# Hybrid trunk layer on one core: the joint turns of two up-projection pairs placed behind the product of the third quarter

## The chip, the cores and the metric

The kernel runs on one core of one Trainium2 chip. The metric is the device time of one execution in microseconds (us). The core's engines are TensorE (PE, with its weight loads, PEld, as a row of their own), VectorE (DVE), ScalarE (ACT), GpSimd (POOL) and SyncE (SP, which issues most DMAs). Each has its own queue and runs it in order; they wait for each other through semaphores.

## The reference

One layer of a trunk on 256 tokens of width 2048: a norm, a gated delta rule and a pooling mixer behind one input projection, an output projection, and then a feed-forward part. The change is in the feed-forward part's up projection.

```python
h = rmsnorm(x, norm_ffn_w[l])
gate, up = jnp.split(jnp.einsum('bsd,df->bsf', h, w_up[l]), 2, axis=-1)      # w_up: 2048 x 2*5632
gate = causal_dwconv(gate, conv_ffn_w[l]) + conv_ffn_b[l]                    # three taps over the tokens
x = x + jnp.einsum('bsf,fd->bsd', jax.nn.gelu(gate, approximate=False) * up, w_down[l])
...
return rmsnorm(x, norm_final_w)
```

## The kernel before

**Numbers.** Every float32 weight tile (128 partitions x 2 x 512) is split in two tiles of a shorter type: a high half, cast by ScalarE (`whi`, L318), and a low half, the difference, made by VectorE (`wlo`, L329). Activations are split in the same way. A product of two such operands is three matmuls: high with high, high with low, low with high.

**Tiling of the up projection.** The 5632 columns are 11 chunks of 512 (`c` = 0 to 10), each with a gate half and an up half: a pair. For each pair there are four results of 128 tokens x 512 columns: `bank[col, t]`, column half `col` (0 gate, 1 up) and token half `t`. The contraction of 2048 is eight steps `kp` of 256. In a "plain" step one weight tile meets both token halves, twelve matmuls. A "group" replaces four plain steps (two `kp`, gate and up), which are eight quarter products of six matmuls each, by seven such products on sums of weight quarters and sums of activation quarters. Its products are named 11, T1, T2, 21, T3, 22 and T4. Pairs 1 to 7 and 9 have two groups each (chunks in `TWO`); pairs 8 and 10 have one.

**How the seven products share results.** Some results are begun as copies or sums of others. T1 has a bank of its own ("own"), which ScalarE copies out. When 21 is reached, VectorE adds `bank[0, 1]` and "own" into `bank[1, 0]` (L1438); T3 accumulates into that same `bank[0, 1]`; behind T3 VectorE adds `bank[0, 1]` and "own" again into `bank[1, 1]` (L1459). Product 22 goes into `bank[1, 0]`, T4 into `bank[1, 1]`, 21 into `bank[0, 0]`. The matmuls of products and plain steps are all at L1423.

**Turns.** When the last plain step of a column half is done, ScalarE copies its two banks to an `e` tile (L1473 for gate, L1476 for up). The "turns" of chunk `c` are 16 transposes on TensorE (L1485), eight of the gate `e` and eight of the up `e`, each into a two-bank tile of the pool `psm` (two tiles). Then `gate_part` runs the three taps on the turned gate (L1370 on ScalarE, L1375 on VectorE) and the Gelu, and `up_part` multiplies with the turned up (L1391) and splits the result.

**What sets the order.** TensorE's order is written out by hand: the list `up_steps`, built pair by pair, is walked under a manual schedule for PE. While chunk `c` ends, the group of chunk `c + 1` begins: its products stand between the last up steps (`rest`) of chunk `c`, and the turns of chunk `c` stand among them. The queues of the other engines follow from a scheduler and from the order in which the work is issued. Up to three `whi` and three `wlo` tiles are alive, four raw weight tiles, and four banks of the pool `psg`.

Of the kernel before, what the change touches and what calls it, by code (L numbers as in the profile page):

```python
# [36 lines left out]
def kernel(  # L37
# [63 lines left out]
    up_steps = []  # L101
    TAIL = 3
    for c in range(NUP):
        kps = [kp for kp in range(KD // 2) if kp // 2 not in chunks_of[c]]
        gate_steps, up_only = ([("plain", c, col, kp) for kp in kps] for col in range(2))
        tail = min(6, len(kps)) if c + 1 in TWO else TAIL
        up_steps += gate_steps[:tail]
        for a, b in zip(gate_steps[tail:], up_only):
            up_steps += [a, b]
        rest = up_only[-tail:]  # L110
        if c + 1 == NUP:
            up_steps += rest
            break
        parts = [[("part", c + 1, what, ch) for what in UP_PARTS] for ch in chunks_of[c + 1]]
        if len(rest) == 4:
            up_steps += [rest.pop(0)]
        up_steps += [("loads", c + 1)]
        if c + 1 in TWO:
            first_four = [parts[ch][n] for ch in range(2) for n in (0, 1)] + [parts[ch][2] for ch in range(2)]
            if len(rest) == 3:  # L120
                rest = rest[:2] + [None] + rest[2:] + [None, None]
            for a, b in zip(first_four, rest):
                up_steps += [a, b] if b else [a]
            p21, t3, p22, t4 = ([parts[ch][n] for ch in range(2)] for n in range(3, 7))
            up_steps += p21 + t3 + p22 + [("turns", c)] + t4
        else:
            t1, p11, t2, p21, t3, p22, t4 = parts[0]
            up_steps += [t1, rest[0], p11, rest[1], t2, rest[2], p21, t3, p22, ("turns", c), t4]
    for step in up_steps:
        if step[0] == "plain":  # L130
            srcs.append(up_w[step[1]][step[2]][step[3]])
# [1438 lines left out]
    for hf in range(2):  # L1570
# [11 lines left out]
        for n, step in enumerate(steps[hf]):  # L1582
# [9 lines left out]
            if step[0] == "plain":  # L1592
                kp, c = step[1], step[2] % 2
# [147 lines left out]
```

## Time and profile before

| | |
|---|---|
| median of 3 runs | 1536.62 us (1535.81 to 1536.63) |
| profiled execution | 1536.34 us |
| its span | 1534.6 us |
| granted TensorE clock, mean | 0.998 |
| busy: PE, PEld, DVE, ACT | 99%, 82%, 81%, 57% of the span |
| 16 transposes of a chunk (L1485) | 64 matmuls for the chunks 6 to 9 between 1100 and 1300 us |

The span is what the profiler saw of the one execution; 1.74 us lie outside it. Times in rows are microseconds from the span's start. In a row of the timeline stand start, duration, engine, line, operation, output and inputs; in square brackets, where there are any, the engine's idle time just before and what ended it. A duration of several merged instructions (x4) goes from the first one's start to the last one's end. The rows of a weight load show best when TensorE turns to the next product.

### The profile page before, as it was taken

What the parts mean: (1) busy time and instruction counts of PE and PEld (TensorE: products, weight loads), DVE (VectorE), ACT (ScalarE), POOL (GpSimd) and SP (SyncE); (2) the same over time, 40 slices, a digit from 0 to 9 for tenths busy, and PEclk for the clock granted to TensorE, in tenths of its full rate; (3) what the DMA queues carried; (4) which work ended last, traced back from release to release, by engine and by line L of the source; (5) the groups of instructions that cost most, each with busy time, mean ns of one, the idle gap of its engine ahead of it and who ended that gap; (6) DMA issues with size and microseconds to landing.
All of it is one profiled execution on the core that took longest, in us unless ns stands there. A gap on an engine that the chain in (4) does not pass through costs nothing.

```text
span 1534.6 us, 20205 instructions
## 1 busy us (share of the span) xinstructions
PE 1522.4 (99%) x7290; PEld 1255.5 (82%) x7290; DVE 1235.9 (81%) x1729; ACT 871.3 (57%) x1126; POOL 71.5 (5%) x97
## 2 busy tenths in 40 slices
PE   9999999999999999999999999999999999999997
PEld 8878888788888888788888888888888888888876
DVE  6779758885589757877667999999998886989896
ACT  6455446454556446454455676666766665555553
POOL 1000000000000001000000000000000011010200
PEclk9999999999999999999999999999999999999999
DMA  8777658776667656766578646666456568566662
GB/s 278 208 228 211 191 152 232 223 201 172 199 213 218 186 160 208 231 192 192 177 259 302 197 163 216 219 208 218 151 188 210 150 219 264 173 220 209 235 203 97
DMA packets 170098, 313.61 MB, mean 204 GB/s; under 512 B 23650, under 2 KB 27010, under 8 KB 169870
## 3 DMA queue, kind: packets, MB, share of 16 engines
q1 hardware_dynamic: 160864, 283.17, 59.3%
q0 software_dynamic: 7344, 27.27, 5.4%
q10 hardware_dynamic: 1790, 1.89, 0.4%
q8 instruction: 57, 0.93, 0.3%
q14 instruction: 43, 0.35, 0.1%
HBM read 303.33 MB, written 8.95 MB: 203 GB/s over the span
## 4 chain that ended last, share of the span: by engine, by line
PE 98%; DVE 1%; issue 0%; ACT 0%; DMA 0%; POOLq 0%; POOL 0%; SPq 0%; DVEq 0%; ACTq 0%
PE psg L1423 28%; PE psm L368 15%; PE psm L366 15%; PE psm L367 15%; PE psm L1408 7%; PE psg L1408 7%; PE psm L1423 2%; PE psm L512 1%; PE psm L1485 1%; PE psg L411 1%; PE psg L899 1%; DVE wlo L329 0%; PE psg L901 0%; ACT whi L318 0%; PE psg L1037 0%
## 5 line engine op out<-in xcount | busy, mean ns | idle before, releaser
L318 ACT CAST whi<-raw 128x1024 fp32r<-128x1024 f32 x420 | 440.7, 1052 | 408.3 <-PE psm L367 252.2
L329 DVE TENSOR_TENSOR wlo<-raw,whi 128x1024 fp32r<-128x1024 f32 x418 | 509.8, 1224 | 166.8 <-ACT whi L318 160.6
L318 ACT CAST whi<-quad 128x1024 fp32r<-128x1024 f32 x182 | 191.1, 1054 | 140.5 <-PE psg L1423 46.4
L329 DVE TENSOR_TENSOR wlo<-quad,whi 128x1024 fp32r<-128x1024 f32 x182 | 221.2, 1223 | 28.8 <-ACT whi L318 27.5
L368 PE MATMUL psm<-wlo,xhl 128*128 128x512 f32 x432 | 170.2, 394 | 0.2 <-DVE wlo L329 0.2
L366 PE MATMUL psm<-whi,xhl 128*128 128x512 f32 x432 | 169.0, 391 | 0.0
L367 PE MATMUL psm<-whi,xhl 128*128 128x512 f32 x432 | 168.6, 390 | 0.0
L1423 PE MATMUL psg<-whi,fhl 128*128 128x512 f32 x504 | 127.2, 390 | 0.0
L1423 PEld LDWEIGHTS psg<-whi,fhl 128*128 128x128 f32 x504 | 94.4, 188 | 19.5
L368 PEld LDWEIGHTS psm<-wlo,xhl 128*128 128x128 f32 x432 | 81.1, 188 | 17.9 <-DVE wlo L329 1.1
L367 PEld LDWEIGHTS psm<-whi,xhl 128*128 128x128 f32 x432 | 81.1, 188 | 16.6
L366 PEld LDWEIGHTS psm<-whi,xhl 128*128 128x128 f32 x432 | 81.2, 188 | 16.5
L245 DVE TENSOR_TENSOR quad<-quad,quad 128x1024 f32<-128x1024 f32 x72 | 87.9, 1221 | 0.0
L1423 PE MATMUL psg<-wlo,fhl 128*128 128x512 f32 x252 | 69.8, 389 | 0.0
L1423 PE MATMUL psg<-whi,ups 128*128 128x512 f32 x216 | 58.0, 390 | 1.5 <-DVE psg L1438 1.5
L1423 PEld LDWEIGHTS psg<-wlo,fhl 128*128 128x128 f32 x252 | 47.3, 188 | 9.9
L1408 PE MATMUL psm<-whi,hhi 128*128 128x512 f32 (+1 forms) x140 | 54.3, 388 | 0.1
L1408 PE MATMUL psm<-whi,hlo 128*128 128x512 f32 (+1 forms) x140 | 54.1, 386 | 0.0
L1408 PE MATMUL psm<-wlo,hhi 128*128 128x512 f32 (+1 forms) x140 | 53.9, 386 | 0.0
L366 PE MATMUL psm<-whi,mhi 128*128 128x512 f32 x128 | 50.8, 397 | 0.0
L368 PE MATMUL psm<-wlo,mhi 128*128 128x512 f32 x128 | 50.0, 390 | 0.0
L367 PE MATMUL psm<-whi,mlo 128*128 128x512 f32 x128 | 49.9, 390 | 0.0
(439 smaller groups left out, 2918.4 us busy)
## 6 DMA issues: line engine op xcount, KB each, us to landing
raw<-in_w_in_dram SPq DMA_DIRECT2D x224, 512.0 KB, 4.3
raw<-in_w_up_dram SPq DMA_DIRECT2D x104, 512.0 KB, 4.8
quad<-in_w_up_dram SPq DMA_DIRECT2D x72, 512.0 KB, 4.7
raw<-in_w_down_dram SPq DMA_DIRECT2D x56, 512.0 KB, 5.2
raw<-in_w_out_dram SPq DMA_DIRECT2D x32, 512.0 KB, 4.0
quad<-in_w_down_dram POOLq DMA_DIRECT2D x32, 512.0 KB, 5.6
mv<-vrow SPq DMA_DIRECT2D x12, 512.0 KB, 4.8
taps<-in_conv_qkv_w_dram SPq DMA_DIRECT2D x16, 256.0 KB, 5.7
```

The costliest lines, as they stand in the source:

```text
L245: nc.vector.tensor_tensor(out_, plus_, minus_, op=ALU.subtract)
L318: last_cast[0] = nc.scalar.copy(hi, raw).ins
L329: last_split[0] = nc.vector.tensor_tensor(lo, raw, hi.bitcast(F32), op=ALU.subtract).ins
L366: mm(ps[:, t, :], lh(k, t), hi[:, kk, :], start=(k == 0), stop=False)
L367: mm(ps[:, t, :], ll(k, t), hi[:, kk, :], start=False, stop=False)
L368: mm(ps[:, t, :], lh(k, t), lo[:, kk, :], start=False, stop=(k == nk - 1))
L411: nc.tensor.transpose(pt[:, ff, t * P : (t + 1) * P], src[:, t, f * P : (f + 1) * P], ident)
L512: mm(ps_k0[:, t, :], part(k, t), w[:, kk, :], start=(k == 0 and w is hi and part is xh), stop=(k == KD - 1 and w is lo))
L899: mm(pg0, kq[:, h, 0, 0:P], kq[:, h, :, :], start=True, stop=True)
L1408: mm(ps[:, cs], lhs(kk), part_[:, kk, cs], start=(first and kk == 0 and n == 0), stop=(last and kk == 1 and n == 2), skip_group_check=shared)
L1423: mm(ps, lhs(kk), w[n][:, kk], start=(first and n == 0 and kk == 0 and lhs is high), stop=False, skip_group_check=True)
L1485: nc.tensor.transpose(out_[f // 2][:, f % 2, t * P : (t + 1) * P], e[:, t, f * P : (f + 1) * P], ident)
```

## The change

In the two pairs with one group (the chunks 8 and 10) the turns of the chunk before stand directly behind product 21, ahead of T3 and 22. Before they stood behind 22, ahead of T4. The other pairs are as they were. Nothing is added or taken away.

```diff
         else:
             t1, p11, t2, p21, t3, p22, t4 = parts[0]
-            up_steps += [t1, rest[0], p11, rest[1], t2, rest[2], p21, t3, p22, ("turns", c), t4]
+            up_steps += [t1, rest[0], p11, rest[1], t2, rest[2], p21, ("turns", c), t3, p22, t4]
```

What this makes of the queues is shown at the first of the two places, the end of chunk 7 (the second, the end of chunk 9, has the same moves). The rows give line, operation, output and inputs; + is after, - before. On TensorE, from product 21 (bank `psg_10115`) on; `whi_10141` and `wlo_10143` are T3's weights, `whi_10164` and `wlo_10166` those of 22, `whi_10176` before that of T4:

```order
 L1423 MATMUL psg_10115<-whi_10117,fhl_6782 128x512 x4
 L1423 MATMUL psg_10115<-wlo_10119,fhl_6782 128x512 x2
+L1485 MATMUL psm_10176<-ident,e_10044 128x128 x8
+L1485 MATMUL psm_10185<-ident,e_10157 128x128 x8
 L1423 MATMUL psg_10108<-whi_10141,ups 128x512 x4
 L1423 MATMUL psg_10108<-wlo_10143,ups 128x512 x2
 L1423 MATMUL psg_10162<-whi_10164,ups 128x512 x4
 L1423 MATMUL psg_10162<-wlo_10166,ups 128x512 x2
-L1485 MATMUL psm_10202<-ident,e_10044 128x128 x8
-L1485 MATMUL psm_10211<-ident,e_10157 128x128 x8
```

The gate turns (`e_10044`) and the up turns (`e_10157`) moved ahead of T3 and 22; T4 now follows 22 directly.

On VectorE, from the add at 21 on (`wlo` of a quad is T4's low half, those of raw tiles belong to the first two plain steps of chunk 8):

```order
 L1438 TENSOR_TENSOR psg_10162<-psg_10108,own_10082 128x512
-L329 TENSOR_TENSOR wlo_10178<-quad_9926,whi_10176 128x1024
-L1459 TENSOR_TENSOR psg_10186<-psg_10108,own_10082 128x512
-L329 TENSOR_TENSOR wlo_10194<-raw_10190,whi_10192 128x1024
+L329 TENSOR_TENSOR wlo_10198<-quad_9926,whi_10196 128x1024
+L1459 TENSOR_TENSOR psg_10206<-psg_10108,own_10082 128x512
+L1375 SCALAR_TENSOR_TENSOR y_10254<-psm_10176,cfw,y_10254 128x255
+L329 TENSOR_TENSOR wlo_10212<-raw_10208,whi_10210 128x1024
+L1375 SCALAR_TENSOR_TENSOR y_10254<-psm_10176,cfw,y_10254 128x254
 L329 TENSOR_TENSOR wlo_10224<-raw_10220,whi_10222 128x1024
-L1375 SCALAR_TENSOR_TENSOR y_10254<-psm_10202,cfw,y_10254 128x255
-L1375 SCALAR_TENSOR_TENSOR y_10254<-psm_10202,cfw,y_10254 128x254
```

The low half of T4 and the two adds keep their places (only their buffers have other numbers); the first two taps of the gate moved ahead, each before a low half of a plain step.

On ScalarE, from the copies of up `e` on:

```order
 L1476 COPY e_10157<-psg_9840 128x512
 L1476 COPY e_10157<-psg_9884 128x512
-L318 CAST whi_10176<-quad_9926 128x1024
-L318 CAST whi_10192<-raw_10190 128x1024
+L318 CAST whi_10196<-quad_9926 128x1024
+L1370 ACTIVATE y_10254<-psm_10176,vec,cfw 128x256
+L318 CAST whi_10210<-raw_10208 128x1024
 L318 CAST whi_10222<-raw_10220 128x1024
-L1370 ACTIVATE y_10254<-psm_10202,vec,cfw 128x256
```

The first gate activation moved ahead of the high halves of two plain steps. The queues of SyncE and GpSimd keep their order.

## The prediction

> **What bounds the kernel now.** I read the page's first and fourth part first, then the waits of the two TensorE rows, then the chain of waits around each place that the change touches.
>
> ```profile
> span 1534.6 us, 20205 instructions
> ...
> PE 1522.4 (99%) x7290; PEld 1255.5 (82%) x7290; DVE 1235.9 (81%) x1729; ACT 871.3 (57%) x1126; POOL 71.5 (5%) x97
> ...
> PE 98%; DVE 1%; issue 0%; ACT 0%; DMA 0%; POOLq 0%; POOL 0%; SPq 0%; DVEq 0%; ACTq 0%
> ```
>
> TensorE carries 98% of the chain that ends last. So only two things can move the time: TensorE work taken away, or a hole on TensorE filled. The change takes no work away (16 transposes before, 16 after, in each pair). What is left is holes. The waits of matmuls (PE) and of weight loads (PEld), longest first, columns "us in total, times, longest":
>
> ```profile
> PE psg L1423 <- DVE psg L1438: 1.5, 2, 0.7
> ...
> PE psg L1423 <- DVE wlo L329: 0.5, 2, 0.3
> PE psg L1408 <- ACT whi L318: 0.4, 2, 0.2
> ...
> PEld psg L1423 <- DVE psg L1438: 2.3, 2, 1.2
> ```
>
> The largest entry among the matmul waits is one product waiting for the add of L1438, twice. L1438 makes bank[1, 0] from bank[0, 1] and "own" at the product 21; the product T3 then accumulates into the same bank[0, 1], so it must wait until the add has read it. The chain of waits, in order of time, shows where the two are:
>
> ```profile
> 1165.16 1.22 DVE wlo L329
> 1166.38 0.62 DVE psg L1438
> 1167.00 0.04 issue
> 1167.05 3.02 PE psg L1423 x12
> 1170.07 1.75 PE psm L1485 x16
> ...
> 1253.98 0.62 DVE psg L1438
> 1254.60 0.04 issue
> 1254.65 3.02 PE psg L1423 x12
> 1257.67 1.75 PE psm L1485 x16
> ```
>
> Both holes are in the two pairs of this change (chunks 8 and 10; the turns of L1485 there are those of chunks 7 and 9), two products ahead of the turns. The reader should see that the turns need nothing of this add: they read only the evicted e tiles.
>
> **The size of a hole.** I go by the starts of weight loads. The timeline of the first place (start, duration, engine, line; p21 is the load at 1164.55, T3 at 1167.04, 22 at 1168.31, the turns at 1169.67, T4 at 1171.54, the first plain product of chunk 8 at 1172.81):
>
> ```profile
> 1164.55 0.87 PEld L1423 LDWEIGHTS psg<-whi,fhl 128*128 128x128 f32 x4
> 1165.02 1.07 ACT L1476 COPY e<-psg 128x512 f32<-128x512 f32 x2
> 1165.98 1.06 ACT L318 CAST whi<-quad 128x1024 fp32r<-128x1024 f32 x1
> 1166.30 0.69 DVE L1438 TENSOR_TENSOR psg<-psg,own 128x512 f32<-128x512 f32 x1
> 1167.04 0.77 PEld L1423 LDWEIGHTS psg<-whi,ups 128*128 128x128 f32 x4 [1.17 <-DVE psg L1438]
> 1167.07 1.22 DVE L329 TENSOR_TENSOR wlo<-quad,whi 128x1024 fp32r<-128x1024 f32 x1
> 1168.28 1.05 ACT L318 CAST whi<-raw 128x1024 fp32r<-128x1024 f32 x1 [1.24 <-PE psg L1423]
> 1168.31 0.87 PEld L1423 LDWEIGHTS psg<-whi,ups 128*128 128x128 f32 x4
> 1168.74 0.70 DVE L1459 TENSOR_TENSOR psg<-psg,own 128x512 f32<-128x512 f32 x1 [0.45 <-PE psg L1423]
> 1169.36 2.59 DVE L329 TENSOR_TENSOR wlo<-raw,whi 128x1024 fp32r<-128x1024 f32 x2
> 1169.67 1.90 PEld L1485 LDWEIGHTS psm<-ident,e 128*128 128x128 f32 x16
> 1170.98 0.56 ACT L1370 ACTIVATE y<-psm,vec,cfw 128x256 f32<-128x256 f32 x1 [0.28 <-PE psm L1485]
> 1171.54 0.76 PEld L1423 LDWEIGHTS psg<-whi,fhl 128*128 128x128 f32 x4
> 1172.81 1.80 PEld L1423 LDWEIGHTS psg<-whi,fhl1a 128*128 128x128 f32 x8
> ```
>
> An undisturbed product of six matmuls holds TensorE for 1169.67 - 1168.31 = 1.36 us; the 16 turns for 1171.54 - 1169.67 = 1.87; the product right behind the turns for 1172.81 - 1171.54 = 1.27. From p21 to the first plain product TensorE takes 1172.81 - 1164.55 = 8.26 us. With p21 1.36, turns 1.87, T3 1.27, 22 1.36 and T4 1.36 it is 7.22. The hole is worth 1.04 us. The same stretches of the second place, p21, then T3 with its hole, the turns and T4 (us, PE busy, clock, DMA share, GB/s):
>
> ```profile
> 1252.15:1253.51 1.36, 1.36 (x7) 1.00 0.83 259
> 1253.51:1255.91 2.40, 1.65 (x7) 1.00 0.64 222
> ...
> 1257.27:1259.14 1.87, 1.87 (x17) 1.00 0.85 285
> 1259.14:1260.41 1.27, 1.27 (x9) 1.00 0.78 247
> ```
>
> They are equal to the first place to the hundredth: 2.40 where 1.36 was due, 1.04 again. The granted clock is 1.00 in all of them, so nothing comes or goes by the clock.
>
> A rule on how to read such a gap: the Trainium skill, "Perfetto Trace Analysis", section "Identifying the Most-Contended Engine", says that matmul busy time misjudges TensorE because matmuls are pipelined, and that weight-load busy time is the better measure. The two wait rows bear it out in part: matmul idle gives 1.5 us for both places, weight-load idle 2.3, the distance between starts 2.08. By that page alone the gain would be 2.3 and the time 0.2 lower than mine; the starts decide, because a load that follows a stall or the turns is 0.09 us shorter (1.27 against 1.36).
>
> **The change step by step.** *Turns ahead of T3, on TensorE:* they start when p21 is through, 1164.55 + 1.36 = 1165.91, and end at 1167.78. The add of L1438 is done at 1166.30 + 0.69 = 1166.99, and a load follows it 0.05 later (1167.04). So T3 finds its bank free 0.74 us early: the hole is gone, -1.04 in each pair. *What the turns themselves need:* gate e is old; the two copies of up e (L1476) end at 1165.02 + 1.07 = 1166.09, and the up turns, the second eight of 16, start at 1165.91 + 1.87/2 = 1166.85. Spare 0.76: no wait, 0.
>
> *What is late next: T4.* Before, the turns stood between 22 and T4 and covered L1459, the add that makes T4's bank from T3's result. That cover is gone. L1459 starts 1168.74 - 1167.04 = 1.70 after T3's load and takes 0.70. T3 now loads at 1167.78, L1459 runs 1169.48 to 1170.18, T4 may load at 1170.23. Its turn comes at 1167.78 + 1.27 + 1.36 = 1170.41. Spare 0.18: cost 0, but this is the tightest point of the forecast. L1459 cannot be held by VectorE: ahead of it stands only T4's low half, which is done at 1167.07 + 1.22 = 1168.29.
>
> *VectorE and ScalarE, new places in the queues.* On ScalarE y0 (L1370) now stands ahead of the first plain product's high half. It starts 1170.98 - 1169.67 = 1.31 after the turns, so at 1167.22, ends at 1167.78, while the high half behind it waits anyway until T3 has released its buffer: 1.24 after T3's load (1168.28 - 1167.04), so 1169.02. Cost 0. On VectorE one tap (L1375) now stands ahead of the first plain low half: L1459 ends 1170.18, the tap (0.48) 1170.66, the low half about 1171.85. TensorE loads that product at 1170.41 + 1.36 = 1171.77, and its low matmuls come 1.8 us into it (the row at 1172.81 loads eight high weights first), at 1173.57. Spare 1.7: cost 0. The row for the tap's length, and the rows for the loads:
>
> ```profile
> L1375 DVE SCALAR_TENSOR_TENSOR y<-psm,cfw,y x37: 474/478/484, 1099.8 to 1268.2; 128x254 f32<-128x254 f32 x19, 128x255 f32<-128x255 f32 x18
> ...
> 1170.62 30.73 SPq L224 DMA_DIRECT2D raw<-in_w_up_dram  x10
> ...
> 1183.94 1.98 PE L1423 MATMUL psg<-whi,fhl 128*128 128x512 f32 x8
> ...
> DMA to landing us min/median/max: 3.6/4.7/6.5
> ```
>
> *The SyncE queue.* Its order is unchanged, and no step issues a DMA, but the load issued at 1170.62, behind the first plain low half, refills that product's buffer for the fifth plain product (the matmul at 1183.94, so its load about 1183.7). It is issued about 1.25 us later now and wanted 1.04 earlier. Landing at 1171.9 + 6.5 = 1178.4 at the latest of these rows; wanted, with one cast of 1.05, by 1183.7 - 1.04 - 1.05 = 1181.6. Spare 3.2 us: cost 0. GpSimd's order does not change.
>
> *Sum:* 2 x -1.04 = -2.08 us. The profiled execution took 1536.34 us, 1.74 outside its span of 1534.6; it becomes a span of 1532.5 and 1534.26 in all. The median of the runs (1536.62) is 0.28 above the profiled one; against it the sum gives 1534.54, and I predict 1534.5. Everything behind 1173 only moves up with TensorE, which paces it.
>
> Bounds of what the trace before does not show, T4 directly behind 22: best, the whole -2.08; a little more if the shift also shortens one of the later small waits (I allow 0.3 for run to run); worst, T4 waits for L1459 a whole VectorE low half (1.22) longer, less its spare of 0.18, which is 1.04 and takes the gain away. The row nearest to the new order is L1459's own start 0.45 after VectorE fell idle, so I take no wait.
>
> **Rivals.** (1) T4 takes the wait over. For it: 0.18 us of spare. Against it: VectorE is idle ahead of L1459, so nothing can push it. From 0.18 of lateness on it costs one for one, at 1.22 nothing is left: 1534.6 to 1536.6. (2) The up turns wait for the copies of up e. Against it: 0.76 of spare; it needs a high-half cast (1.06) to slip ahead of the copies, for a loss of 0.3 in each pair: 1535.1. (3) Slower: the refill for the fifth plain product, issued later and wanted earlier, makes its cast late and TensorE waits. Issued at 1171.9 and wanted by 1181.6, it starts to cost when the load takes 9.7 us, gives no change at 10.7, and at 12.3 in both pairs (2.6 lost in each, 1.04 won) the kernel is at 1539.7. The longest of 37 loads took 6.5, so this wants a queue about twice as slow. (4) More than the sum: gate work that starts earlier also removes later waits, for below 1533.5; against it, the later matmul waits quoted above hold 0.5 + 0.4 us together, which is 1533.6 with all of them gone.
>
> **How the numbers follow.** Chances: the sum holds (within 0.4 us of 1534.5) 0.77; rival 1 0.09; rival 2 0.04; rival 3, or an unforeseen loss of that size, 0.04; rival 4 0.06. A measurement of this kernel can tell about 0.2%, 3.1 us, from no change; the sum is 0.135%. So within 0.2%: 0.77 + 0.09 + 0.04 = 0.90; faster by more 0.06; slower by more 0.04. The range runs from the fastest run less the sum (1535.81 - 2.08 = 1533.7, and 0.1 for spread) to 1536.7, where rival 1 has eaten everything.
>
> **What the changed profile would show.** Right: no waits for L1438 in either wait view; 7.2 us, not 8.26, from p21's first load to the first plain product in both pairs; T3 right behind the turns; VectorE idle some 1.2 us, not 0.45, ahead of L1459; the span near 1532.5. Wrong: a wait of T4 for L1459 (rival 1), of the turns for L1476 (rival 2), of a cast for a raw load about 14 us behind T3 with TensorE idle after it (rival 3). If the two stretches are 7.2 us and the span is not shorter, a wait further on gave the time back, and my claim that TensorE paces all that follows was the wrong step.

## The result and the profile after

| | before | after |
|---|---|---|
| median of 20 runs each | 1536.41 us (1535.48 to 1537.42) | 1533.84 us (1533.35 to 1534.79) |
| ratio, after to before | | 0.9985, 95% interval 0.9979 to 0.9991 |
| profiled execution | 1536.34 us | 1533.53 us |

By the medians the change is worth 2.57 us, by the ratio 2.3; the interval, times 1536.41, reaches from 1.4 to 3.2 us. The forecast was 2.08 us less and 1534.5 us. Faster, then, by 0.15%: less than the 0.2% that the prediction thought could be told from no change, but with 20 runs each the interval leaves out 1. In two later series one execution took far longer than all others (3121 us of the kernel before, 2573 us of the kernel with all pairs); without them the medians given below move by less than 0.1 us.

The lines of the page of the changed kernel that answer to those of before:

```profile
span 1531.8 us, 20205 instructions
...
PE 1521.9 (99%) x7290; PEld 1256.6 (82%) x7290; DVE 1235.4 (81%) x1729; ACT 871.7 (57%) x1126; POOL 71.1 (5%) x97
...
PE 98%; issue 0%; DVE 0%; ACT 0%; POOL 0%; POOLq 0%; ACTq 0%; DVEq 0%
```

The counts are the same, and the busy times differ by 0.5 us for matmuls and VectorE and by 1.1 us for weight loads; the span is 2.8 us shorter. No work went away, so idle time did. VectorE's share of the chain fell from 1% to 0%. All waits of matmuls that the view still lists (us in total, times, longest):

```profile
PE psm L427 <- POOL ones L417: 1.1, 1, 1.1
PE psg L1408 <- ACT whi L318: 0.4, 2, 0.2
PE psm L368 <- DVE wlo L329: 0.2, 1, 0.2
```

The largest entry of before in the up projection, 1.5 us for L1438, is gone, and none for L1459 or L1476 has come. (Two small entries of before are missing too, L1423 for low halves and L512 for a cast; both lie ahead of the two places and come and go between executions of the same code.) The chain of waits through the first place (start, duration, what) shows it as one unbroken run of TensorE:

```profile
1159.83 5.90 PE psg L1423 x26
1165.73 1.75 PE psm L1485 x16
1167.48 14.52 PE psg L1423 x64
```

Before, the add of L1438 stood in this chain as a link of 0.62 us between p21 and T3. The rows of the timeline that bear on the first place, others left out (p21 loads at 1163.97, the turns at 1165.34, T3 at 1167.21, 22 at 1168.47, T4 at 1169.83, the first plain product at 1171.19):

```profile
1163.97 0.87 PEld L1423 LDWEIGHTS psg<-whi,fhl 128*128 128x128 f32 x4
1164.44 1.07 ACT L1476 COPY e<-psg 128x512 f32<-128x512 f32 x2
1165.34 1.91 PEld L1485 LDWEIGHTS psm<-ident,e 128*128 128x128 f32 x16
1165.72 0.69 DVE L1438 TENSOR_TENSOR psg<-psg,own 128x512 f32<-128x512 f32 x1
1166.64 0.56 ACT L1370 ACTIVATE y<-psm,vec,cfw 128x256 f32<-128x256 f32 x1 [0.19 <-PE psm L1485]
1167.21 0.76 PEld L1423 LDWEIGHTS psg<-whi,ups 128*128 128x128 f32 x4
1168.47 0.87 PEld L1423 LDWEIGHTS psg<-whi,ups 128*128 128x128 f32 x4
1168.89 0.70 DVE L1459 TENSOR_TENSOR psg<-psg,own 128x512 f32<-128x512 f32 x1 [1.18 <-PE psg L1423]
1169.50 0.47 DVE L1375 SCALAR_TENSOR_TENSOR y<-psm,cfw,y 128x255 f32<-128x255 f32 x1
1169.83 0.87 PEld L1423 LDWEIGHTS psg<-whi,fhl 128*128 128x128 f32 x4
1171.19 1.77 PEld L1423 LDWEIGHTS psg<-whi,fhl1a 128*128 128x128 f32 x8
```

The add runs from 1165.72 to 1166.41, wholly beside the turns, and no weight load has a bracket behind it: no wait of TensorE is listed. From p21 to the first plain product it is 1171.19 - 1163.97 = 7.22 us, where it was 8.26. The second place by stretches (us, PE busy; the columns are those of before): p21, the turns, T3, 22 and T4:

```profile
1250.48:1251.84 1.36, 1.36 (x8) 1.13 (x6) 0.76 (x1) 1.36 (x3) 0.64 (x1) 1.00 0.76 253
1251.84:1253.71 1.87, 1.87 (x17) 1.77 (x16) 1.79 (x3) 1.68 (x3) 0.72 (x1) 1.00 0.82 269
1253.71:1254.97 1.26, 1.26 (x8) 1.06 (x7) 0.51 (x1) 0.03 (x2) 0.45 (x1) 1.00 0.69 241
1254.97:1256.33 1.36, 1.36 (x7) 1.13 (x6) 0.93 (x2) 1.05 (x2) 0.28 (x1) 1.00 0.83 295
1256.33:1257.69 1.36, 1.36 (x7) 1.13 (x6) 1.36 (x3) 1.06 (x2) 0.00 (x0) 1.00 0.75 241
```

TensorE is busy through each of them, at a granted clock of 1.00; they sum to 7.21 us.

**Where the 2.8 us of the spans come from.** Two stretches give 1.04 + 1.05 = 2.09. Another 0.58 is there before the place is reached (1163.97 against 1164.55), in instructions that both kernels issue in the same order; the rest is 0.1. The 0.58 is a balance of small waits that differ in both directions: just ahead of 963 us the changed kernel was still 0.3 us behind. The largest difference after that is one wait 200 us ahead of the place, the weight load of one low half, first in the kernel before, then in the changed one:

```profile
962.97 0.30 PEld L1423 LDWEIGHTS psg<-wlo,ups 128*128 128x128 f32 x2 [0.72 <-DVE wlo L329]
```

```profile
962.82 0.30 PEld L1423 LDWEIGHTS psg<-wlo,ups 128*128 128x128 f32 x2 [0.22 <-DVE wlo L329]
```

It is 0.5 us shorter there, without any edit near it; a second one at 1049 us is 0.3 shorter (0.65 and 0.32). In nine traces of kernels whose work up to this place is the same (these two, and seven of the runs below) p21 loads between 1163.76 and 1165.56. Half a microsecond between two spans therefore says nothing of the change, and the stretch itself has to be read.

### The profile page after: what moved, and what is told of

It reads as the page before. It is cut to its first block, busy times and chain, and to the rows that moved or that the text cites. A ratio compares the mean times of both kernels' runs of the same rounds, so it can differ in the third digit from the quotient of the medians.

```text
span 1531.8 us, 20205 instructions
## 1 busy us (share of the span) xinstructions
PE 1521.9 (99%) x7290; PEld 1256.6 (82%) x7290; DVE 1235.4 (81%) x1729; ACT 871.7 (57%) x1126; POOL 71.1 (5%) x97
## 4 chain that ended last, share of the span: by engine, by line
PE 98%; issue 0%; DVE 0%; ACT 0%; POOL 0%; POOLq 0%; ACTq 0%; DVEq 0%
PE psg L1423 28%; PE psm L368 15%; PE psm L366 15%; PE psm L367 15%; PE psm L1408 7%; PE psg L1408 7%; PE psm L1423 2%; PE psm L512 1%; PE psm L1485 1%; PE psg L411 1%; PE psg L899 1%; PE psg L901 0%; PE psm L427 0%; PE psg L1037 0%; PE psg L1045 0%
## 5 line engine op out<-in xcount | busy, mean ns | idle before, releaser
L1423 PE MATMUL psg<-whi,fhl 128*128 128x512 f32 x504 | 126.9, 389 | 0.0
L1423 PEld LDWEIGHTS psg<-whi,fhl 128*128 128x128 f32 x504 | 94.6, 188 | 19.7
L1423 PE MATMUL psg<-wlo,fhl 128*128 128x512 f32 x252 | 69.8, 389 | 0.0
L1423 PE MATMUL psg<-whi,ups 128*128 128x512 f32 x216 | 57.9, 390 | 0.0
L1423 PEld LDWEIGHTS psg<-wlo,fhl 128*128 128x128 f32 x252 | 47.3, 188 | 9.8
```

The costliest lines, as they stand in the source:

```text
L1423: mm(ps, lhs(kk), w[n][:, kk], start=(first and n == 0 and kk == 0 and lhs is high), stop=False, skip_group_check=True)
```

## The experiments

All edits below are against the changed kernel unless said otherwise, and stand in the line that orders a pair with one group. The theories: **H**, the change fills the hole behind L1438, 1.04 us in each of two pairs, and nothing else; **G**, it helps because the turns, and with them the gate's work, start earlier; **R**, the 0.58 us ahead of the place belong to the change; **K**, the adds are not what T3 and T4 wait for; **L**, T3 waits for its own weights.

### The kernel before again

No edit to the kernel before.

> The kernel before, unchanged, for a second trace and a null comparison. Theory H (the gain is the hole that the add of L1438 left on TensorE, 1.04 us in each of two pairs): ratio 1.000, TensorE waits for L1438 twice again, and the stretch from product 21 to the first plain product is 8.26 us in both pairs. The trace of the changed kernel reached product 21 of the first place 0.58 us earlier, ahead of any moved instruction; H says that this differs from run to run by some tenths. Rival R (those 0.58 us belong to the change): this trace reaches the place at 1164.55 again, within 0.1.

1536.06 us against 1536.08 for the kernel before, ratio 1.0001 (0.9992 to 1.0009). Both stretches took 8.26 us again, and L1438 is waited for twice, 1.5 us of matmul idle as before. The place was reached at 1164.74, 0.19 later than in the first trace of the same code, where R allowed 0.1. What is stable to the hundredth is the stretch; what is not is when it begins.

### The new order in one of the two pairs

```
-             up_steps += [t1, rest[0], p11, rest[1], t2, rest[2], p21, ("turns", c), t3, p22, t4]
+             up_steps += [t1, rest[0], p11, rest[1], t2, rest[2]] + (
+                 [p21, ("turns", c), t3, p22, t4] if c + 1 == 8 else [p21, t3, p22, ("turns", c), t4])
```

> The move in the pair of chunk 8 alone; chunk 10 keeps the old order. H: half of the sum, -1.04 us against the kernel before; the first stretch 7.22 us, the second 8.26, one wait for L1438 left of 0.75 us. Rival G (the gain comes from gate work that starts earlier and relieves something later in the up projection): the first pair is followed by three more pairs and the second by none, so nearly all of the gain, -2 us or more.

1535.27 against 1536.08, ratio 0.9995 (0.9987 to 1.0004): 0.8 us by medians where 1.04 was due, too little to be told from nothing by the time alone. The trace decides. The first stretch took 7.21 us, the second 8.26, with T3's load there:

```profile
1253.87 0.76 PEld L1423 LDWEIGHTS psg<-whi,ups 128*128 128x128 f32 x4 [1.17 <-DVE psg L1438]
```

Each pair gains by itself, and the hole stays where the order stayed. The view of the matmul waits names L1438 twice in this trace, not once: the other wait, 0.66 us at 958.03, is a T3 in a pair with two groups, where nothing was moved and the weight load waited 1.05 us for a cast. No other trace here has it.

### The turns one place later, behind T3

```
-             ... p21, ("turns", c), t3, p22, t4]
+             ... p21, t3, ("turns", c), p22, t4]
```

> The turns one product later than in the change: behind T3, ahead of 22. Gate work starts 1.36 us earlier than before, but T3 still stands directly behind 21. H: no change against the kernel before (within 0.2 us), both stretches 8.26 us, both waits for L1438 stay at 0.75. G: more than half of the gain of the change, -1.2 us or more.

1536.65 against 1536.08, ratio 1.0001 (0.9992 to 1.0010). The turns start one product earlier than in the kernel before, and nothing is gained: both stretches take 8.25 us, and T3 waits as before:

```profile
1168.05 0.76 PEld L1423 LDWEIGHTS psg<-whi,ups 128*128 128x128 f32 x4 [1.17 <-DVE psg L1438]
```

G, by which an earlier start of the turns should itself help, falls.

### T4 directly behind T3

```
-             ... p21, ("turns", c), t3, p22, t4]
+             ... p21, ("turns", c), t3, t4, p22]
```

> The change, and the products 22 and T4 exchanged, so that nothing stands between T3 and T4 (the second add, L1459). H: the hole comes back in another place: T4 loads 1.70 + 0.70 + 0.05 = 2.45 us after T3 instead of 1.27, the stretch is 1.36 + 1.87 + 2.45 + 1.27 + 1.36 = 8.31 us, so +0.1 us against the kernel before for both pairs (1536.5 where that takes 1536.4). Rival K (the adds are not what T3 and T4 wait for, or the second one is covered in another way): as the change, -2.1 us or more.

1536.35 against 1536.08, ratio 1.0001 (0.9993 to 1.0010): the gain is gone. This is the case of the prediction's first rival. The view of the waits and T4's load:

```profile
PE psg L1423 <- DVE psg L1459: 1.6, 2, 0.8
```

```profile
1169.43 0.76 PEld L1423 LDWEIGHTS psg<-whi,fhl 128*128 128x128 f32 x4 [1.22 <-DVE psg L1459]
```

T4 loads 1169.43 - 1167.00 = 2.43 us after T3 (2.45 expected), and both stretches take 8.31 us, to the hundredth what was expected. So the add behind T3 (L1459) makes a hole of the same kind as the one behind 21, and product 22 alone is what covers it in the changed kernel. K falls.

### The old order, with the add ahead of 22's low half

Against the kernel before: in the two pairs VectorE makes the low half of 22's weights only behind the newest add. (One line is added, so the add is L1439 here, the products L1424.)

```
+                 if src in (("up", 8, "22", 0), ("up", 10, "22", 0)):
+                     behind_conv.enter_context(tc.issue_after(last_sum[0]))
                  last_split[0] = nc.vector.tensor_tensor(lo, raw, hi.bitcast(F32), op=ALU.subtract).ins
```

> The kernel before, its turns in the old place; in the two pairs VectorE makes the add of L1438 ahead of the low half of 22 instead of behind it. H: the hole shrinks because the add ends earlier: it can start when the first copy of up e is out (about 1165.65 in the old trace), so T3 loads 0.64 us earlier in each pair: stretches 7.6 us instead of 8.26, -1.3 us in all, a wait for L1438 left that is a third as long. Rival L (T3 waits for its own weights, and the add is named only because it ends last): stretches stay at 8.26, no change.

1534.95 against 1536.20, ratio 0.9992 (0.9983 to 1.0000), 1.25 us by medians where 1.3 was expected; stretches of 7.60 and 7.64 us against an expected 7.6. The add and T3's load (p21 loads at 1165.38):

```profile
1166.46 0.70 DVE L1439 TENSOR_TENSOR psg<-psg,own 128x512 f32<-128x512 f32 x1 [1.55 <-ACT e L1477]
...
1167.21 0.76 PEld L1424 LDWEIGHTS psg<-whi,ups 128*128 128x128 f32 x4 [0.51 <-DVE psg L1439]
```

The add starts 1.08 us after p21's load, not 1.75, and T3's load moves by just that: L falls. It also shows why no order on VectorE can close the hole: VectorE then stood idle for 1.55 us until ScalarE had copied out up e, which frees a bank for the add's result. The order on TensorE could close it: the turns do not need the add, and the up turns, which do need the copies, come only behind the gate turns.

### The gate turns behind 21, the up turns behind 22

The list has `("turns", c, 0)` behind p21 and `("turns", c, 1)` behind p22, and the step of the turns makes one column half at a time.

> Only the eight gate turns behind 21, the eight up turns stay behind 22. H, by the starts of the old trace: the gate turns end at 1165.91 + 0.95 = 1166.86, T3 still waits for the add until 1167.04, then 1.27, 1.36, the up turns 0.95, T4 1.27: the stretch is 7.35 us with 0.2 us of wait for L1438 left in each pair; L1459 is covered by 22 and the up turns. Rival L: 8.26.

One execution, 1534.19 us, span 1532.5. The two stretches took 7.38 and 7.37 us, expected 7.35. The first, from p21 to T4:

```profile
1164.30 0.87 PEld L1423 LDWEIGHTS psg<-whi,fhl 128*128 128x128 f32 x4
...
1165.66 1.03 PEld L1485 LDWEIGHTS psm<-ident,e 128*128 128x128 f32 x8
...
1166.04 0.69 DVE L1438 TENSOR_TENSOR psg<-psg,own 128x512 f32<-128x512 f32 x1
...
1166.79 0.76 PEld L1423 LDWEIGHTS psg<-whi,ups 128*128 128x128 f32 x4
...
1169.42 1.03 PEld L1485 LDWEIGHTS psm<-ident,e 128*128 128x128 f32 x8
1170.42 0.76 PEld L1423 LDWEIGHTS psg<-whi,fhl 128*128 128x128 f32 x4
```

Eight turns behind 22 hold TensorE for 1170.42 - 1169.42 = 1.00 us; from those behind 21 to T3 it is 1.13. T3 loads 0.06 us after the add's end at 1166.73, so it still comes 0.13 us too early for the add, a wait that is too short for the views to list. Eight of the 16 turns do most of the work: 0.88 of the 1.04 us. The second eight are hardly needed in the hole; they only must not cost more elsewhere.

### The turns one place earlier, ahead of 21

```
-             ... rest[2], p21, ("turns", c), t3, p22, t4]
+             ... rest[2], ("turns", c), p21, t3, p22, t4]
```

> In the two one-group pairs the turns stand one place further ahead, in front of product 21. H (a hole is filled by whatever is ready; rival 2 of the prediction gets its case here): the gate half of the turns runs at once, the up half needs the second copy of up e (L1476), which ends 2 x 1.07 / 2 + 0.47 = 1.54 us after rest's end, and the gate half takes 0.94, so TensorE waits about 0.65 us for L1476 in each pair. 21, T3, 22 and T4 then follow without a wait for either add: L1438 does not hang on 21 and is done 2.44 us after rest's end, where T3's turn comes at 3.8. From rest's end to the first plain product 0.65 + 1.87 + 1.27 + 3 x 1.36 = 7.87 us, against 7.22 with the change and 8.26 before: half a gain, -0.4 in each pair, span about 1533.6 if the place is reached at the usual time. K (the adds are not what T3 and T4 wait for): 7.2 us as with the change, no wait for L1476.

One execution, 1535.99 us, span 1534.3; it reached the place 1.2 us later than the changed kernel's trace, so again the stretch is what counts: 7.82 and 7.84 us, from the turns' first load at 1165.19 to the first plain product at 1173.01 (7.87 expected). The rows of the first place:

```profile
1165.66 1.06 ACT L1476 COPY e<-psg 128x512 f32<-128x512 f32 x2
...
1166.77 0.75 PEld L1485 LDWEIGHTS psm<-ident,e 128*128 128x128 f32 x7 [0.35 <-ACT e L1476]
...
1169.81 1.23 DVE L329 TENSOR_TENSOR wlo<-quad,whi 128x1024 fp32r<-128x1024 f32 x1 [2.19 <-ACT whi L318]
...
1170.95 0.69 DVE L1459 TENSOR_TENSOR psg<-psg,own 128x512 f32<-128x512 f32 x1
...
1171.76 0.76 PEld L1423 LDWEIGHTS psg<-whi,fhl 128*128 128x128 f32 x4 [0.30 <-issue]
```

The up turns wait for the copies of up e, as the second rival had it: the turns take 1167.49 - 1165.19 = 2.30 us in place of 1.87, 0.43 of waiting where I had expected 0.65. A second wait that I had not expected makes up for it, so that 7.82 for 7.87 is luck in part. T4's low half comes late on VectorE, because its high half is cast late (at 1168.72, when ScalarE had waited 1.54 us for product 21); it stands ahead of L1459, and pushes that add to 2.20 us behind T3's load in place of 1.70. T4 loads at 1171.76, 0.12 after the add's end at 1171.64 and 0.26 later than its turn (1170.14 + 1.36 = 1171.50). The view calls this gap "issue" and does not name the add; that it is the add is read from the times, not from a releaser. So one place earlier is too early (0.42 to 0.44 us gained in each pair in place of 1.04), one place later is too late.

### The changed kernel again, and the new order in all pairs

The second of these also puts the turns ahead of T3 in the pairs with two groups:

```
-             up_steps += p21 + t3 + p22 + [("turns", c)] + t4
+             up_steps += p21 + [("turns", c)] + t3 + p22 + t4
```

> The changed kernel, unchanged, beside the others of this series. H: 2.08 us less than the kernel before (about 1534.3 where that takes 1536.4), no wait for L1438 or L1459, both stretches 7.22 us; the place where product 21 of the first pair starts lies anywhere between 1163.8 and 1165.6, as in the six traces so far, since nothing ahead of it is changed. Rival R (part of the measured 2.57 is made ahead of the two pairs): it starts near 1163.97 again, and the gain is 2.5 us or more.

> The change, and the same move in the eight pairs with two groups as well (turns behind the two products 21). The traces before and after show no wait of TensorE for L1438 there. H: no further gain, as the change within 0.5 us (-2.1 us against the kernel before), since there is no hole to fill. Rival G (turns that come earlier help by themselves): several tenths more in each of the eight pairs, -4 us or more. Some casts, taps and loads change places too, so a loss of some tenths would not speak for either.

On one chip: the changed kernel 1534.03 against 1536.20, ratio 0.9987 (0.9979 to 0.9996), 2.17 us by medians, with stretches of 7.22 and 7.21 and no wait for L1438 or L1459; all pairs 1536.47, ratio 1.0001 (0.9992 to 1.0010). The changed kernel's second trace reaches the first place at 1164.15, and its gain is below R's 2.5 us. Both its traces are there ahead of both traces of the kernel before (1164.55 and 1164.74), but the kernel with the new order in the pair of chunk 8, whose work is the same up to there, came at 1164.88: R falls.

Between the two kernels of this series I had expected no difference beyond 0.5 us; the second is 2.4 us slower, and its shortest execution (1535.41) is longer than the longest of the other (1535.20). That expectation was wrong. The trace of the second reaches the first place at 1167.41, 1.85 us later than the latest of the nine. The waits of the weight loads between 860 and 1160 us, where the pairs with two groups lie, and one of the four places:

```profile
PEld psg L1423 <- DVE wlo L329: 3.4, 4, 0.9
```

```profile
1094.28 0.47 DVE L1375 SCALAR_TENSOR_TENSOR y<-psm,cfw,y 128x255 f32<-128x255 f32 x1
1094.67 1.22 DVE L329 TENSOR_TENSOR wlo<-quad,whi 128x1024 fp32r<-128x1024 f32 x1
...
1095.80 0.48 DVE L1375 SCALAR_TENSOR_TENSOR y<-psm,cfw,y 128x254 f32<-128x254 f32 x1
1096.19 1.22 DVE L329 TENSOR_TENSOR wlo<-raw,whi 128x1024 fp32r<-128x1024 f32 x1
...
1097.32 1.22 DVE L329 TENSOR_TENSOR wlo<-quad,whi 128x1024 fp32r<-128x1024 f32 x1
...
1098.59 0.30 PEld L1423 LDWEIGHTS psg<-wlo,fhl 128*128 128x128 f32 x2 [0.85 <-DVE wlo L329]
```

The earlier turns release the first two taps (L1375), and these now go ahead of low halves on VectorE; each delays what follows by 0.39 us (1094.28 to 1094.67). The low half that ends at 1097.32 + 1.22 = 1098.54 is then late, and the load that needs it, that of a T4, waits 0.85. The low half of a plain step (1096.19) has gone ahead of it as well; in the kernel before, at this place, it stood behind the low halves of both T4. All four waits are those of a T4, the product that the turns stood ahead of before. In the ten traces of kernels that keep the turns there in these pairs, no load of a T4 waits in this window. So the turns behind 22 had covered T4's low halves. They had also covered L1459 once: at 1009.59 the load of a T4 waits 0.52 us, 0.12 behind the end of that add, and the view again says "issue".

In the pairs with one group the same move of a tap cost nothing. One difference is VectorE's load, in the kernel before, by stretches of 100 us (us; PE, PEld, DVE, ACT and POOL busy):

```profile
900.00:1000.00 100.00, 99.70 (x457) 82.65 (x456) 96.91 (x100) 69.01 (x81) 0.00 (x0) 1.00 0.53 179
1000.00:1100.00 100.00, 99.78 (x465) 82.95 (x464) 96.76 (x102) 67.44 (x79) 0.00 (x0) 1.00 0.58 198
```

With 97% there is no room there for 0.8 us of taps ahead of needed work. Around the first place of the change, from 1155 to 1180, VectorE is busy for 20.7 of 25 us, 83%; around the one pair with two groups that lies behind it (chunk 9, no such wait), from 1180 to 1240, for 53.0 of 60 us, 88%. Another difference stands in the kernel: for the turns of the chunks 0 to 6 it issues each new high and low half behind the newest gate activation and tap (L306, L1379), for the later ones not. No run separates the two.

### All pairs, with the taps behind the newest low half

```
-            with tc.issue_after(last_sum[0]) if c < NUP - 1 else ExitStack():
+            with tc.issue_after(last_split[0] if c in (0, 1, 2, 3, 4, 5, 6, 8) else last_sum[0]) if c < NUP - 1 else ExitStack():
                 for j in (1, 0):
```

> Turns ahead of T3 in the two-group pairs too, as in the kernel with all pairs, but in those pairs each tap on VectorE (L1375) is put behind the newest low half (L329) issued at that point, so that the first two taps no longer stand ahead of low halves that TensorE needs next. The first kernel with all pairs was about 2.4 us slower than the change, with four matmul waits for low halves (1.7 us) and four such waits of weight loads (3.4 us) between 860 and 1160, where the change has one (0.3). Theory V (the taps that became ready earlier went ahead of needed low halves on a VectorE that is 97% busy there): those waits shrink to one or two, below 1 us of weight-load idle, and the time is within 0.6 us of the change, 1534.0 to 1534.6. Rival D (the turns behind 22 covered something else in those pairs: the add L1459 ahead of T4, or the loads whose order moved): the waits stay or turn into waits for L1459 or for a cast, and the time stays near 1536.4. A gain beyond the change would show holes in the two-group pairs that the wait views do not list: I expect none.

1535.26 against 1536.42, ratio 0.9993 (0.9984 to 1.0002). That is neither: 0.7 us above what theory V allowed, 1.1 below D. By medians, each against its own runs of the kernel before, the two kernels with all pairs stand at +0.27 and -1.16 us and the changed kernel at -2.17. But the interval of the middle one overlaps with both others, so the time alone shows neither the step of 1.4 nor that of 1.0. The trace shows more:

```profile
PEld psg L1423 <- DVE wlo L329: 1.9, 4, 0.7
...
1135.13 0.30 PEld L1423 LDWEIGHTS psg<-wlo,ups 128*128 128x128 f32 x2 [0.57 <-DVE wlo L329]
...
1138.00 0.30 PEld L1423 LDWEIGHTS psg<-wlo,fhl1b 128*128 128x128 f32 x2 [0.27 <-DVE wlo L329]
```

Of the four waits, those at 883 and 1099 are gone. At the two other places, 967 and 1053, 0.71 us are left of 0.77 and 0.33 of 0.93. So theory V holds in full at two of the four places. The remaining two waits of the 1.9 us are the rows above. The first is of a product 22 and says nothing of the new order: the same load waits 0.76 us with T4 directly behind T3, where the pairs with two groups keep the old order.

```profile
1133.10 0.30 PEld L1423 LDWEIGHTS psg<-wlo,ups 128*128 128x128 f32 x2 [0.76 <-DVE wlo L329]
```

The second is again of a T4, and at 922.77 a T4 waits 0.52 us, 0.12 behind the end of L1459. So rival D is right in part: with the taps held back, the turns' cover of 1.87 us is still missing ahead of T4. The place of chunk 8 is reached at 1165.58, which is no sign of a loss: the nine traces go up to 1165.56. What the taps and the lost cover are each worth in time stays open.

No kernel of these runs is shown to beat the changed one; the kernel with eight turns behind 21, run once (1534.19), lies among its executions.

## Why the prediction was right

- **The size of the hole.** Forecast 1.04 us in each place, 7.22 us where 8.26 stood. Measured 7.22 and 7.21, and 7.22 and 7.21 in the second trace. The hole comes back whole where the old order is kept in one pair, and shrinks with the add's start where only that is moved (0.66 and 0.62 us shorter stretches for an add that starts 0.67 earlier).
- **How to read it.** Matmul idle said 1.5 us for both places, weight-load idle 2.3, the distance between starts 2.08. The stretches became 2.09 shorter: neither idle time was the loss, and 2.09 lies between them. The Trainium skill, "Perfetto Trace Analysis", section "Identifying the Most-Contended Engine", advises the busy share of weight loads (and the share of peak matmul work), not that of matmuls, to judge how close TensorE is to its roofline. It gives no price for a single gap; to read 2.3 us out of it went further than the page does.
- **The turns' own needs.** Forecast spare for the up turns 0.76. The copies of up e end at 1164.44 + 1.07 = 1165.51, and half of the turns later it is 1165.34 + 0.94 = 1166.28: 0.77. The case with the turns one place earlier shows the wait that the spare keeps off.
- **T4, the tightest point.** Forecast spare 0.18, VectorE idle 1.2 ahead of L1459. Measured idle 1.18; L1459 ends at 1169.59, its load may follow 0.05 later, T4's turn is 1169.83: spare 0.19. The rival that T4 takes the wait over is real as a mechanism (8.31 us with T4 directly behind T3) and was rightly judged not to apply.
- **ScalarE and VectorE.** Forecast y0 1.31 after the turns; measured 1166.64 - 1165.34 = 1.30. Its cost was 0, as the tap's (1169.50, behind L1459) was. This "0" held by its spare, forecast 1.7 us and measured 1.9 (the low half is done at 1171.10, its load comes at 1173.00), and not as a rule: in the pairs with two groups taps that moved ahead in the same way made two loads of T4 wait for 0.8 us.
- **The refill for the fifth plain product.** Neither wait view has any entry between 1171 and 1310 us; the rival by a late load did not occur.
- **The sum.** -2.08 forecast; -2.57 and -2.17 by the medians of two comparisons. The measured 1533.84 is 0.66 below the forecast 1534.5, more than the 0.4 that the prediction allowed around its sum, and not as low as its rival 4 (below 1533.5). Of that, 0.2 is the median of before, which came out at 1536.41 and not 1536.62. The rest, 0.5 more gain than the sum, lies inside the interval (1.4 to 3.2 us), and no run shows a cause for it. The two profiled executions show no later wait removed (rival 4): of the span's 2.8 us, 2.09 are the stretches and 0.58 lie ahead of any moved instruction. The second comparison fits the sum, and 0.8 for one pair does not speak against it. So the mechanism is confirmed by the stretches, to 0.01 us, and the total only within its interval.

## What to carry to other kernels

When one engine carries nearly the whole chain, look for the few waits that its own order causes, and put behind the instruction that starts another engine's work something that needs none of it. Price the hole by the distance between the starts of the same two instructions with and without it, and price the place that loses its cover by the same rows; both were right here to 0.02 us. The same move cost 2.4 us in the pairs with two groups, most of which lie where VectorE was 97% busy: work that became ready earlier was also issued earlier, ahead of what was needed, and the product that lost its cover had no spare. Price each place anew.

## What the hardware showed that was not expected

- Turning between products and transposes costs something each time: 16 turns in a row hold TensorE for 1.87 us, eight for 1.00, so each further turn takes 0.87 / 8 = 0.109 and 0.13 are paid once. The product behind gets 0.1 back (1.26 against 1.36), so that 0.03 are left.
- The same instructions in the same order reached the same place up to 1.8 us apart (1163.76 with T4 directly behind T3, 1165.56 with the turns behind T3), while the stretch of 40 matmuls behind it repeated to 0.01 us, at both places and in both traces, in the kernel before (8.26) and in the changed one (7.22 and 7.21).
- Gaps of 0.30 us (turns ahead of 21) and 0.52 us (all pairs) that the times put down to an add on VectorE were shown as "issue", without a releaser; in each the load followed the add's end by 0.12 us.
